# Fox attention scores for two heads at a time: three 64-row products per head on the two halves of the partitions

## The chip, the cores and the metric

The kernel runs on one core of a Trainium2 chip. The metric is the device time of one execution in microseconds (us); lower is better. The engines are named as the profile names them: PE is TensorE's matmuls and PEld its weight loads, DVE is VectorE, ACT is ScalarE, POOL is GpSimd, SP issues most of the transfers.

## What is computed

Two layers of a first block and one second block work on 512 tokens of 1024 features, all in float32. The change touches the attention of the first layer alone, which has 16 heads of 64 features and a forget gate:

```python
def _fox_attention(x, w_in, b_f, w_out):
    proj = x @ w_in
    q, k, v = ...                       # 16 heads of 64
    c = cumsum(log_sigmoid(f_logit))    # one running sum per head
    logits = einsum('bhqd,bhkd->bhqk', qb, k) * HEAD_DIM ** -0.5
    logits = logits + cb[..., :, None] - c[..., None, :]
    p = softmax(where(kpos <= qpos, logits, -inf))
    o = einsum('bhqk,bhkd->bhqd', p, v)
    return merge(o) @ w_out
```

Every product is made of float32 values split into a rounded part (hi) and the rest (lo), and leaves out the product lo x lo. So a product of two split operands has three terms: hi hi, hi lo, lo hi.

## The kernel before

The features lie on the partitions. `qk(pair)` projects q and k of two heads at once (48 matmuls of 512 columns, lines L217 to L219), so that head A lies on partitions 0 to 63 of the result and head B on 64 to 127. `qk_stack1` (L527) then makes three operands of the full height for each head: A holds q_hi on one half of the partitions and q_lo on the other, B holds k_hi on both halves, Ck holds k_lo on one half and zeros on the other. These zeros are set once by `zero_halves` (L506). A head takes three ACT and two DVE instructions of 64 partitions for it (L533 to L537).

`scores` (L540) is then two matmuls of the full 128 rows: A times B gives hi hi and lo hi together (L543), A times Ck gives hi lo (L544). There are four tiles of 128 queries; the keys of a tile are the causal ones, at least 256: 256, 256, 384 and 512 columns.

`fox_front` makes a head's gate row (L550, ACT copy L553, DVE sum L554), its scores, the row minima on DVE (L566, L569), the exponentials on ACT (L571) and the normalisation (L577 to L582). `fox_back` makes the transposes of the probabilities (L401), splits them (L193 on ACT, L194 on DVE) and multiplies with the values (L594, L595); `combine` (L604, L605) adds the two halves of its result.

The loop over heads in `fox` weaves the front of head h with the back of head h - 1. Projections for the next pair, the values (L291 to L293) and the first half of the output projection stand in the same program. A scheduler that is part of the build sets the order of the instructions on each engine from that program; the engines then run their queues in that order. Scores, gate rows and transposes use four PSUM banks in turns (`at`, 4 buffers), the product with the values uses one (`ms`), the projections three (`mm`). Inputs of the weight split are loaded by SP in chunks (`raw`, 3 buffers) and split by ACT and DVE (L185, L186).

`setup_cols` (L111) loads the small vectors into a staging tile `st`, transposes it (L156) and copies it to `cols`; this runs beside the first projections.

Of the kernel before, what the change touches and what calls it, by code (L numbers as in the profile page):

```python
# [15 lines left out]
S = 512  # L16
# [15 lines left out]
def constants():  # L32
    """Arrays that depend on shapes alone."""
# [36 lines left out]
def weave(*gens):  # L70
    """Runs generators step by step, in turns."""
    gens = [g for g in gens if g is not None]
    while gens:
        for g in list(gens):
            try:
                next(g)
            except StopIteration:
                gens.remove(g)


class K:
# [29 lines left out]
    def setup_cols(self):  # L111
# [26 lines left out]
        with self.tc.tile_pool(name="stage", bufs=1) as sp:  # L138
            r = 0
            st = None  # L140
            for name, ap, m in vecs:
                self.col[name] = r
                done = 0
                while done < m:
                    if r % P == 0:
                        st = sp.tile([P, P], F32, tag="st", name="st")
                        if total - r < P:
                            nc.vector.memset(st, 0.0)
                    k = min(m - done, P - r % P)
                    nc.sync.dma_start(st[r % P:r % P + k, :], ap[done * P:(done + k) * P].rearrange("(m p) -> m p", p=P))  # L150
                    done += k
                    r += k
                    if r % P == 0 or r == total:
                        b = (r - 1) // P
                        pt = self.psa()
                        nc.tensor.transpose(pt[:, :P], st, self.ident)  # L156
                        nc.vector.tensor_copy(self.cols[:, b * P:(b + 1) * P], pt[:, :P])
        # the gate of block 2's convolution takes halves
# [13 lines left out]
    def wchunk(self, src):  # L172
        """src [nk*128, cols] in DRAM, or a list of such to lie side by side; returns hi and lo tiles [128, nk, cols]."""
# [26 lines left out]
    def ws_load(self, W, c0, cols=256, ktiles=KD):  # L200
        """Chunks of W[:, c0:c0+cols] over K."""
# [19 lines left out]
    def ws_pairs(self, gc, vc, first):  # L221
        """Two pairs of products; the first ones after a new x^T by halves of the tokens."""
# [101 lines left out]
    def to_T(self, src, t):  # L324
        """src [128 tokens, 1024] -> xT[:, k, t*128:(t+1)*128]."""
# [30 lines left out]
    def rstd(self, var, eps, scale=1.0):  # L356
        """(var * scale + eps) ** -0.5 for a [128, n] tile."""
# [8 lines left out]
    def layer_norm(self, t, G, B, jk):  # L366
        """In place on x[:, t]; the row sums of its parts are in self.sums[t]; jk is scratch [128, 512]."""
# [15 lines left out]
    def res_epi(self, c0, n, scale, part=None, after=None):  # L383
        """x = scale * x + product; with part the row sums go to that column of self.sums."""
# [11 lines left out]
    def pT_split(self, Pt, j, t_from, pool, bufs=3):  # L396
        """Transposes of block column j of Pt[t] [128 q, keys] for t >= t_from, split into hi and lo."""
# [10 lines left out]
    def p_tile(self, pool, bufs=2):  # L408
        """Causal tiles of probabilities: for query tile t the keys up to (t + 1) * 128."""
# [4 lines left out]
    def fox(self, pool):  # L414
# [4 lines left out]
        # operands of the negated scores: [q_hi; q_lo], [k_hi; k_hi], [k_lo; 0] for each head of a pair  # L419
        Ck = self.zero_halves(pool)  # L420
# [13 lines left out]
        def qk(pair):  # L434
# [3 lines left out]
            o = self.qk_stack(qp, kp, pool, Ck, pair % 2)  # L438
            ops[2 * pair], ops[2 * pair + 1] = o
# [9 lines left out]

        def oproj(half, post=None):  # L450
# [3 lines left out]
        fx = [pool.tile([P, 1280], F32, tag="Pt", name="Pt", bufs=2) for _ in range(2)]  # L454
# [6 lines left out]
        # the first values and the forget gates' logits  # L461
# [9 lines left out]
        # v = log sigmoid; c = its running sum over the tokens  # L471
# [11 lines left out]
        self.setup_cols()  # L483
        prev = None
        for h in range(17):
            if h < 16:
                if h % 2 == 0 and h < 14:
                    qk(h // 2 + 1)
                if h in (1, 5, 9):
                    vproj(h // 4 + 1)  # L490
                Pt = self.p_tile(pool)
                cur = self.fox_front(pool, ops[h], h, sel, cst, causal, Pt)
            else:
                cur = None
            weave(cur, prev)
            prev = back(h, Pt) if h < 16 else None
            if h == 15:
                oproj(0)
        G, B = self.bcast(I["ln_attn_g"][0], "Pt", pool, 1280, 2), self.bcast(I["ln_attn_b"][0], "Pt", pool, 1280, 2)
        oproj(1, self.norm_post(G, B, pool.tile([P, S], F32, tag="NC", name="NC")))  # L500

# [7 lines left out]
    def log1pexp(self, a, b, c, d):  # L509
        """b = log(1 + exp(-|a|)); c, d scratch."""  # L510
# [36 lines left out]
    def fox_front(self, pool, ops, h, sel, cst, causal, Pt):  # L547
        nc = self.nc
        bp = self.psa()
        nc.tensor.matmul(bp, sel[:, h:h + 1].to_broadcast([P, P]), cst, start=True, stop=True)  # L550
        NC = pool.tile([P, S], F32, tag="NC", name="NC", bufs=1)
        BM = pool.tile([P, S], F32, tag="BM", name="BM", bufs=1)
        nc.scalar.activation(NC, bp, AF.Copy)  # L553
        nc.vector.tensor_tensor(out=BM.rearrange("p (t k) -> p t k", t=NT), in0=NC.rearrange("p (t k) -> p t k", t=NT),  # L554
                                in1=causal.rearrange("p (o k) -> p o k", o=1).to_broadcast([P, NT, P]), op=ALU.add)
        m1 = self.sm.tile([P, 4], F32, tag="m1", name="m1")
        m2 = self.sm.tile([P, 4], F32, tag="m2", name="m2")
        s4 = self.sm.tile([P, 4], F32, tag="s4", name="s4")
        yield
        for t in range(NT):  # L560
            n = (t + 1) * P
            sp = self.scores(ops, t, max(256, n))
            d = slice(t * P, n)
            init = -LOWEST
            if t:
                nc.vector.tensor_tensor_reduce(out=Pt[t][:, :t * P], in0=sp[:, :t * P], in1=NC[:, :t * P], scale=1.0, scalar=-LOWEST,  # L566
                                               op0=ALU.add, op1=ALU.min, accum_out=m1[:, t:t + 1])
                init = m1[:, t:t + 1]
            nc.vector.tensor_tensor_reduce(out=Pt[t][:, d], in0=sp[:, d], in1=BM[:, d], scale=1.0, scalar=init,  # L569
                                           op0=ALU.add, op1=ALU.min, accum_out=m2[:, t:t + 1])  # L570
            nc.scalar.activation(Pt[t], Pt[t], AF.Exp, scale=-1.0, bias=m2[:, t:t + 1], accum_out=s4[:, t:t + 1])  # L571
            yield
        self.normalise(Pt, s4)
# [25 lines left out]
    def combine(self, op, of, e, pool):  # L599
        """of rows of head e = upper + lower half of op."""  # L600
# [9 lines left out]
    def out_proj(self, W, k0, kt, xh, xl, scale, post=None):  # L610
        """x = scale * x + (rows k0.. of the product); the last part goes on to post(t)."""
# [12 lines left out]
    def xsn(self, groups, ktiles, xh, xl, k0=0):  # L624
        """As xs for groups (W, c0, epi) of 512 columns, by token tiles."""
# [122 lines left out]
    def softmax_exp(self, ops, Pt, mask):  # L748
        """Pt = exp(scores - max); returns 1 / sum."""
# [12 lines left out]
    def diff_front(self, ops1, ops2, mask, nlam, P1, P2, s1):  # L762
        """P1 = exp1 - lambda * sum1 / sum2 * exp2, which is sum1 times the difference; s1 gets the sums of exp1."""
# [9 lines left out]
    def diff_back(self, pool, P1, V, sg, oT, s1):  # L773
# [4 lines left out]
        for j in range(NT):  # L778
# [6 lines left out]
            if j == NT - 1:  # L785
                # o is s1 times the head's output
# [724 lines left out]
```

## Time and profile before

| | before |
|---|---|
| time, median of 3 runs | 2128.2 us (2127.27 to 2129.58) |
| profiled execution, first to last instruction (span) | 2127.1 us |
| PE busy | 2080.3 us, 98% |
| PEld busy | 1791.1 us, 84% |
| DVE busy | 1318.6 us, 62% |
| ACT busy | 1021.9 us, 48% |
| first and last gate row of the Fox heads (L550) start at | 63.6 and 228.2 us |

The profiled execution has no other time of its own than its span; the median of the runs is 1.1 us above it. "Busy" of PE counts matmuls until their modelled ends, which reach into the next matmul, so the step from one start to the next start, not the length of one matmul, says what a matmul costs on PE.

### The profile page before, as it was taken

What the parts mean: (1) busy time and instruction counts of PE and PEld (TensorE: products, weight loads), DVE (VectorE), ACT (ScalarE), POOL (GpSimd) and SP (SyncE); (2) the same over time, 40 slices, a digit from 0 to 9 for tenths busy, and PEclk for the clock granted to TensorE, in tenths of its full rate; (3) what the DMA queues carried; (4) which work ended last, traced back from release to release, by engine and by line L of the source; (5) the groups of instructions that cost most, each with busy time, mean ns of one, the idle gap of its engine ahead of it and who ended that gap; (6) DMA issues with size and microseconds to landing.
All of it is one profiled execution on the core that took longest, in us unless ns stands there. A gap on an engine that the chain in (4) does not pass through costs nothing.

```text
span 2127.1 us, 29643 instructions
## 1 busy us (share of the span) xinstructions
PE 2080.3 (98%) x11499; PEld 1791.1 (84%) x11499; DVE 1318.6 (62%) x2522; ACT 1021.9 (48%) x1880; POOL 74.3 (3%) x109
## 2 busy tenths in 40 slices
PE   8999999999999999999999998999999999999998
PEld 7888888898898788888998887877898778888887
DVE  5777876536636888775536547897798554332334
ACT  4777554314425987444324434676475343222322
POOL 0000000000000000010000001000000010000000
PEclk9999999999999999999999999999999999999999
DMA  6221233232323121252323323211323425232322
GB/s 167 61 60 60 70 126 109 92 97 80 107 82 100 50 70 60 65 165 79 102 87 109 94 91 106 70 30 35 104 61 96 138 94 172 87 104 84 114 92 72
DMA packets 206018, 193.82 MB, mean 91 GB/s; under 512 B 9029, under 2 KB 187446, under 8 KB 205878
## 3 DMA queue, kind: packets, MB, share of 16 engines
q1 hardware_dynamic: 199942, 173.04, 27.1%
q0 software_dynamic: 4928, 15.22, 2.3%
q10 hardware_dynamic: 1008, 3.67, 0.5%
q8 instruction: 91, 1.49, 0.3%
q14 instruction: 49, 0.40, 0.1%
HBM read 185.61 MB, written 6.29 MB: 90 GB/s over the span
## 4 chain that ended last, share of the span: by engine, by line
PE 51%; DVE 3%; ACT 1%; POOL 1%; issue 1%; POOLq 0%; DVEq 0%; ACTq 0%
PE mm L217 10%; PE mm L218 10%; PE mm L219 10%; PE mm L292 2%; PE mm L293 2%; PE mm L291 2%; PE mm L259 2%; PE mm L257 2%; PE mm L258 2%; PE at L1171 1%; PE at L259 1%; PE at L257 1%; PE at L401 1%; PE at L258 1%; DVE wlo L186 1%
## 5 line engine op out<-in xcount | busy, mean ns | idle before, releaser
L186 DVE TENSOR_TENSOR wlo<-raw,whi 128x1024 fp32r<-128x1024 f32 (+4 forms) x336 | 397.7, 1185 | 350.7 <-ACT whi L185 340.9
L217 PE MATMUL mm<-xTh,whi 128*128 128x512 f32 (+1 forms) x1584 | 604.7, 382 | 2.6 <-DVE L L1015 1.2
L219 PE MATMUL mm<-xTh,wlo 128*128 128x512 f32 (+1 forms) x1584 | 604.2, 382 | 0.1
L218 PE MATMUL mm<-xTl,whi 128*128 128x512 f32 (+1 forms) x1584 | 603.7, 381 | 0.0
L185 ACT ACTIVATE whi<-raw 128x1024 fp32r<-128x1024 f32 (+4 forms) x336 | 345.4, 1031 | 509.2 <-PE mm L218 209.4
L217 PEld LDWEIGHTS mm<-xTh,whi 128*128 128x128 f32 x1584 | 298.3, 188 | 57.6 <-issue 3.1
L219 PEld LDWEIGHTS mm<-xTh,wlo 128*128 128x128 f32 x1584 | 298.2, 188 | 56.1 <-DVE wlo L186 0.3
L218 PEld LDWEIGHTS mm<-xTl,whi 128*128 128x128 f32 x1584 | 298.5, 188 | 54.5 <-DVE xTl L194 0.2
L825 DVE SCALAR_TENSOR_TENSOR cy<-mm,cols,cy 128x511 f32<-128x511 f32 (+1 forms) x172 | 128.6, 748 | 108.4 <-ACT cy L823 105.5
L293 PE MATMUL mm<-whi,hl 128*128 128x256 f32 x528 | 149.4, 283 | 0.0
L292 PE MATMUL mm<-wlo,hh 128*128 128x256 f32 x528 | 149.4, 283 | 0.0
L291 PE MATMUL mm<-whi,hh 128*128 128x256 f32 x528 | 149.4, 283 | 0.0
L292 PE MATMUL mm<-wlo,xTh 128*128 128x256 f32 x416 | 118.4, 285 | 0.9 <-DVE wlo L186 0.9
L291 PE MATMUL mm<-whi,xTh 128*128 128x256 f32 x416 | 118.6, 286 | 0.3 <-ACT xTh L193 0.3
L293 PE MATMUL mm<-whi,xTl 128*128 128x256 f32 x416 | 118.0, 284 | 0.2 <-DVE xTl L194 0.2
L291 PEld LDWEIGHTS mm<-whi,hh 128*128 128x128 f32 x528 | 101.4, 192 | 0.2
L292 PEld LDWEIGHTS mm<-wlo,hh 128*128 128x128 f32 x528 | 101.4, 192 | 0.2
L293 PEld LDWEIGHTS mm<-whi,hl 128*128 128x128 f32 x528 | 101.4, 192 | 0.0
L823 ACT ACTIVATE cy<-mm,cols 128x512 f32<-128x512 f32 x86 | 66.2, 770 | 71.8 <-PE mm L219 71.8
L193 ACT ACTIVATE hh<-cy 128x512 fp32r<-128x512 f32 x66 | 41.1, 623 | 115.8 <-DVE cy L1398 58.9
L292 PEld LDWEIGHTS mm<-wlo,xTh 128*128 128x128 f32 x416 | 80.0, 192 | 1.9 <-DVE wlo L186 1.1
L291 PEld LDWEIGHTS mm<-whi,xTh 128*128 128x128 f32 x416 | 79.9, 193 | 1.5 <-ACT xTh L193 0.8
(422 smaller groups left out, 3580.6 us busy)
## 6 DMA issues: line engine op xcount, KB each, us to landing
raw<-in_ffn_w_in_dram SPq DMA_DIRECT2D x88, 512.0 KB
raw<-in_w_gate_up_dram SPq DMA_DIRECT2D x44, 512.0 KB
raw<-in_w_in_dram SPq DMA_DIRECT2D x40, 512.0 KB
raw<-in_ffn_w_out_dram SPq DMA_DIRECT2D x34, 512.0 KB
raw<-in_a_w_in_dram SPq DMA_DIRECT2D x22, 512.0 KB
raw<-in_w_down_dram SPq DMA_DIRECT2D x20, 512.0 KB
raw<-in_kv_w_dram SPq DMA_DIRECT2D x16, 512.0 KB
raw<-in_ffn_w_out_dram SPq DMA_DIRECT2D x12, 384.0 KB
```

The costliest lines, as they stand in the source:

```text
L185: nc.scalar.activation(hi, raw, AF.Copy)
L186: nc.vector.tensor_tensor(out=lo, in0=raw, in1=hi.bitcast(F32), op=ALU.subtract)
L217: mm(o, wh, a, start=(k == 0), stop=False)
L218: mm(o, wh, b, start=False, stop=False)
L219: mm(o, wl, a, start=False, stop=(k == ktiles - 1))
L257: mm(o, a, hi[:, kk, :], start=(k == 0), stop=False)
L258: mm(o, a, lo[:, kk, :], start=False, stop=False)
L291: mm(o, a, hi[:, kk, :], start=(k == 0 and t % 2 == 0), stop=False)
L292: mm(o, a, lo[:, kk, :], start=False, stop=False)
L293: mm(o, b, hi[:, kk, :], start=False, stop=(k == ktiles - 1 and t % 2 == 1))
L823: nc.scalar.activation(y, ps, AF.Identity, scale=self.c1(f"cw{l}2", m), bias=self.c1(f"cb{l}", m))
L825: nc.vector.scalar_tensor_tensor(out=y[:, o:], in0=ps[:, :S - o], scalar=self.c1(f"cw{l}{j}", m), in1=y[:, o:], op0=ALU.mult, op1=ALU.add)
```

## The change

The two heads of a pair go through `fox_front` together. q and k are split over the full height of 128 partitions into qh, ql, kh, kl, with one ACT and one DVE instruction each for both heads; the stacked operands and the zeros go. A head's scores are three products of 64 rows (qh kh, qh kl, ql kh), written in turns for the upper and the lower half of the partitions, into two PSUM banks. The backs of a pair are woven four steps at a time with the front of the next pair. Probability tiles have four buffers instead of two, gate rows two instead of one, and `setup_cols` uses the tile `of` for staging.

```diff
         def qk(pair):
...
-            o = self.qk_stack(qp, kp, pool, Ck, pair % 2)
-            ops[2 * pair], ops[2 * pair + 1] = o
+            o = ops[pair] = [pool.tile([P, S], F32R, tag=n, name=n, bufs=2) for n in ("qh", "ql", "kh", "kl")]
+            self.split(qp, o[0], o[1], scale=-0.125)
+            self.split(kp, o[2], o[3])
...
+        def backs(p, Pts):
+            for e in range(2):
+                yield from back(2 * p + e, Pts[e])
...
-        for h in range(17):
-            if h < 16:
-                if h % 2 == 0 and h < 14:
-                    qk(h // 2 + 1)
-                if h in (1, 5, 9):
-                    vproj(h // 4 + 1)
-                Pt = self.p_tile(pool)
-                cur = self.fox_front(pool, ops[h], h, sel, cst, causal, Pt)
...
-            weave(cur, prev)
-            prev = back(h, Pt) if h < 16 else None
-            if h == 15:
+        for p in range(9):
+            cur = None
+            if p < 8:
+                if p < 7:
+                    qk(p + 1)
+                if p in (1, 3, 5):
+                    vproj(p // 2 + 1)
+                Pts = [self.p_tile(pool, 4) for _ in range(2)]
+                cur = self.fox_front(pool, ops[p], p, sel, cst, causal, Pts)
+            weave(cur, self.bursts(prev, 4) if prev else None)
+            prev = backs(p, Pts) if p < 8 else None
+            if p == 7:
                 oproj(0)
...
         for t in range(NT):
             n = (t + 1) * P
-            sp = self.scores(ops, t, max(256, n))
+            sps = self.scores2(ops, t, max(256, n))
...
+    def scores2(self, ops, t, nk):
+
+        mm = self.nc.tensor.matmul
+        qh, ql, kh, kl = ops
+        sps = [self.psa(), self.psa()]
+        for i, (a, b) in enumerate(((qh, kh), (qh, kl), (ql, kh))):
+            for e in range(2):
+                r = slice(e * 64, (e + 1) * 64)
+                mm(sps[e][:, :nk], a[r, t * P:(t + 1) * P], b[r, :nk], start=(i == 0), stop=(i == 2))
+        return sps
```

The lines of the changed kernel after L111 stand elsewhere: the transposes are L400, the products with the values L617 and L618, the score products L595.

On PE, at the second head of the first pair, before: the score products (L543, L544; `at` is the score bank) stand between transposes (L401), and each tile has two of them behind each other.

```order
L543 MATMUL at_714<-B_399,A_398 128x256
L544 MATMUL at_714<-Ck10_154,A_398 128x256
L218 MATMUL mm_775<-xTl_77,whi_807 128x512
L401 MATMUL at_705<-ident_85,Pt_536 128x128 x3
L401 MATMUL at_719<-ident_85,Pt_536 128x128 x3
L543 MATMUL at_729<-B_399,A_398 128x256
L544 MATMUL at_729<-Ck10_154,A_398 128x256
L543 MATMUL at_735<-B_399,A_398 128x384
L544 MATMUL at_735<-Ck10_154,A_398 128x384
```

On PE, at the second tile of the second pair, now: `at_857` is the bank of the upper half's head and `at_858` that of the lower half's.

```order
L595 MATMUL at_857<-kh_506,qh_504 128x256
L595 MATMUL at_858<-kh_506,qh_504 128x256
L595 MATMUL at_857<-kl_507,qh_504 128x256
L595 MATMUL at_858<-kl_507,qh_504 128x256
L617 MATMUL ms_806<-ph_849,Vs_160 128x128
L595 MATMUL at_857<-kh_506,ql_505 128x256
L595 MATMUL at_858<-kh_506,ql_505 128x256
```

Here the halves take turns as in the code, with a product of another kind between the second and the third turn.

On PE, at the third tile of the same pair, now: `at_903` is the upper half's head, `at_904` the lower half's.

```order
L595 MATMUL at_903<-kh_506,qh_504 128x384
L595 MATMUL at_903<-kl_507,qh_504 128x384
L595 MATMUL at_903<-kh_506,ql_505 128x384
L218 MATMUL mm_958<-xTh_76,wlo_962 128x512
L216 MATMUL mm_958<-xTh_76,whi_961 128x512
L217 MATMUL mm_958<-xTl_77,whi_961 128x512
L617 MATMUL ms_874<-ph_880,Vs_160 128x512
L218 MATMUL mm_958<-xTh_76,wlo_962 128x512
L216 MATMUL mm_958<-xTh_76,whi_961 128x512
L618 MATMUL ms_874<-pl_881,Vs_160 128x512
L617 MATMUL ms_874<-ph_888,Vs_160 128x384
L595 MATMUL at_904<-kh_506,qh_504 128x384
```

Here the scheduler has moved the three products of the upper half together, and those of the lower half come after seven products of the full height. Behind the Fox stage the order on every engine is that of before.

## Rows read from the trace of the kernel before

**Rows 1.** The page, part 1: busy us (share of the span) xinstructions.

```profile
PE 2080.3 (98%) x11499; PEld 1791.1 (84%) x11499; DVE 1318.6 (62%) x2522; ACT 1021.9 (48%) x1880; POOL 74.3 (3%) x109
```

**Rows 2.** Windows: us, busy (x) of PE, PEld, DVE, ACT, POOL, PEclk, DMA share, GB/s.

```profile
63.60:246.30 182.70, 179.90 (x1097) 154.78 (x1096) 149.31 (x441) 136.69 (x324) 0.54 (x1) 1.00 0.20 59
```

**Rows 3.** Lines of PE, 63.6 to 246.3 us: line, tiles, shapes, count, busy, mean ns, idle before.

```profile
L543 PE MATMUL at<-B,A 128*128 128x256 f32 (+1 forms) x64 | 23.1, 365 | 1.7 <-ACT NC L553 1.6
...
L544 PE MATMUL at<-Ck,A 128*128 128x256 f32 (+1 forms) x64 | 20.7, 324 | 0.0
```

**Rows 4.** Timeline of PE in the first head's scores: start us, us, instruction.

```profile
64.01 0.28 PE L544 MATMUL at<-Ck,A 128*128 128x256 f32 x1
64.12 0.29 PE L543 MATMUL at<-B,A 128*128 128x256 f32 x1
...
64.56 0.34 PE L544 MATMUL at<-Ck,A 128*128 128x384 f32 x1
64.74 0.39 PE L219 MATMUL mm<-xTh,wlo 128*128 128x512 f32 x1
...
65.20 0.39 PE L543 MATMUL at<-B,A 128*128 128x512 f32 x1
65.43 0.40 PE L544 MATMUL at<-Ck,A 128*128 128x512 f32 x1
```

**Rows 5.** Timeline of PEld around a transpose of the first projections.

```profile
40.08 0.19 PEld L217 LDWEIGHTS mm<-xTh,whi 128*128 128x128 f32 x1
40.19 0.19 PEld L218 LDWEIGHTS mm<-xTl,whi 128*128 128x128 f32 x1
```

**Rows 6.** Timeline of PE in block 2: four transposes onto 128, then onto 32 columns.

```profile
1406.22 0.60 PE L947 MATMUL at<-ident,L 128*128 128x128 f32 x4
1406.57 0.48 PE L217 MATMUL mm<-xTh,whi 128*128 128x512 f32 x1
...
1407.35 0.61 PE L1080 MATMUL ms<-ident,L 128*32 128x128 f32 x4
1407.71 0.48 PE L217 MATMUL mm<-xTh,whi 128*128 128x512 f32 x1
```

**Rows 7.** Timeline of PE around the transpose of [rows 5].

```profile
40.08 0.27 PE L156 MATMUL at<-ident,st 128*128 128x128 f32 x1
40.10 0.48 PE L217 MATMUL mm<-xTh,whi 128*128 128x512 f32 x1
40.42 0.40 PE L218 MATMUL mm<-xTl,whi 128*128 128x512 f32 x1
```

**Rows 8.** Waits of PEld, 63.6 to 246.3 us: waiter, releaser, us, times, longest.

```profile
PEld ms L594 <- ACT ph L193: 4.2, 13, 0.7
PEld at L543 <- ACT NC L553: 3.6, 6, 0.8
PEld at L401 <- ACT Pt L580: 2.7, 8, 0.6
PEld ms L595 <- DVE pl L194: 1.3, 5, 0.5
```

**Rows 9.** Lines of DVE and of ACT, 63.6 to 246.3 us.

```profile
L194 DVE TENSOR_TENSOR pl<-at,ph 128x512 fp32r<-128x512 f32 x15 | 10.3, 685 | 0.3 <-ACT ph L193 0.3
...
L534 DVE SCALAR_TENSOR_TENSOR A<-mm,A 64x512 fp32r<-64x512 f32 x12 | 8.3, 689 | 1.6 <-ACT A L533 1.3
L537 DVE TENSOR_TENSOR Ck<-mm,B 64x512 fp32r<-64x512 f32 x12 | 8.3, 689 | 5.4 <-ACT B L536 4.6 <-PE at L401 0.7
...
L193 ACT ACTIVATE ph<-at 128x512 fp32r<-128x512 f32 x15 | 8.8, 590 | 2.2 <-PE at L401 2.2
...
L536 ACT ACTIVATE B<-mm 64x512 fp32r<-64x512 f32 x12 | 7.1, 594 | 0.1
```

**Rows 10.** Lines of DVE and of PE, 0 to 28 us.

```profile
L506 DVE MEMSET Ck<- 128x512 f32 x4 | 1.9, 485 | 0.2
...
L330 PE MATMUL at<-ident,x 128*128 128x128 f32 x32 | 6.5, 389 | 8.7 <-DMA x<-in_x_dram 8.7
```

More of the change, by code (lines that the diff above doesn't have):

```diff
@@ L109, in setup, with setup_cols @@
         nc.vector.memset(self.mhalf, -0.5)
-    def setup_cols(self):
+    def setup_cols(self, pool):
         nc, const, I = self.nc, self.const, self.I
@@ L137, in setup_cols @@
         self.col = {}
[L138 to L157, printed above, removed]
+        r = 0
+        st = None
+        for name, ap, m in vecs:
+            self.col[name] = r
+            done = 0
+            while done < m:
+                if r % P == 0:
+                    st = pool.tile([P, S], F32, tag="of", name="of", bufs=1)[:, :P]
+                    if total - r < P:
+                        nc.vector.memset(st, 0.0)
+                k = min(m - done, P - r % P)
+                nc.sync.dma_start(st[r % P:r % P + k, :], ap[done * P:(done + k) * P].rearrange("(m p) -> m p", p=P))
+                done += k
+                r += k
+                if r % P == 0 or r == total:
+                    b = (r - 1) // P
+                    pt = self.psa()
+                    nc.tensor.transpose(pt[:, :P], st, self.ident)
+                    nc.vector.tensor_copy(self.cols[:, b * P:(b + 1) * P], pt[:, :P])
         i = self.col["c2w0"]
@@ L418, in fox @@
         oT = {}
-        Ck = self.zero_halves(pool)
         Vq, ops, of = {}, {}, {}
@@ L452, in oproj @@
                           1.0 if half else ALPHA, post)
-        fx = [pool.tile([P, 1280], F32, tag="Pt", name="Pt", bufs=2) for _ in range(2)]
+        fx = [pool.tile([P, 1280], F32, tag="Pt", name="Pt", bufs=4) for _ in range(2)]
         v, b, c, d = (fx[1][:, i * 64:(i + 1) * 64] for i in range(4))
@@ L482, in fox @@
         qk(0)
-        self.setup_cols()
+        self.setup_cols(pool)
         prev = None
-        for h in range(17):
-            if h < 16:
-                if h % 2 == 0 and h < 14:
-                    qk(h // 2 + 1)
-                if h in (1, 5, 9):
-                    vproj(h // 4 + 1)
-                Pt = self.p_tile(pool)
-                cur = self.fox_front(pool, ops[h], h, sel, cst, causal, Pt)
-            else:
-                cur = None
-            weave(cur, prev)
-            prev = back(h, Pt) if h < 16 else None
-            if h == 15:
+        for p in range(9):
[10 more added lines that the diff above has]
+            if p == 7:
                 oproj(0)
-        G, B = self.bcast(I["ln_attn_g"][0], "Pt", pool, 1280, 2), self.bcast(I["ln_attn_b"][0], "Pt", pool, 1280, 2)
-        oproj(1, self.norm_post(G, B, pool.tile([P, S], F32, tag="NC", name="NC")))
+        G, B = self.bcast(I["ln_attn_g"][0], "Pt", pool, 1280, 4), self.bcast(I["ln_attn_b"][0], "Pt", pool, 1280, 4)
+        oproj(1, self.norm_post(G, B, pool.tile([P, S], F32, tag="NC", name="NC", bufs=2)))
     def zero_halves(self, pool):
@@ L545, in scores, with fox_front @@
         return sp
-    def fox_front(self, pool, ops, h, sel, cst, causal, Pt):
+    def fox_front(self, pool, ops, pair, sel, cst, causal, Pts):
         nc = self.nc
[L549 to L558, printed above, removed]
+        mm = nc.tensor.matmul
+        NCs, BMs, m1, m2, s4 = [], [], [], [], []
+        for e in range(2):
+            h = 2 * pair + e
+            bp = self.psa()
+            mm(bp, sel[:, h:h + 1].to_broadcast([P, P]), cst, start=True, stop=True)
+            NC = pool.tile([P, S], F32, tag="NC", name="NC", bufs=2)
+            BM = pool.tile([P, S], F32, tag="BM", name="BM", bufs=2)
+            nc.scalar.activation(NC, bp, AF.Copy)
+            nc.vector.tensor_tensor(out=BM.rearrange("p (t k) -> p t k", t=NT), in0=NC.rearrange("p (t k) -> p t k", t=NT),
+                                    in1=causal.rearrange("p (o k) -> p o k", o=1).to_broadcast([P, NT, P]), op=ALU.add)
+            NCs.append(NC)
+            BMs.append(BM)
+            m1.append(self.sm.tile([P, 4], F32, tag="m1", name="m1"))
+            m2.append(self.sm.tile([P, 4], F32, tag="m2", name="m2"))
+            s4.append(self.sm.tile([P, 4], F32, tag="s4", name="s4"))
         yield
@@ L561, in fox_front @@
             n = (t + 1) * P
-            sp = self.scores(ops, t, max(256, n))
+            sps = self.scores2(ops, t, max(256, n))
             d = slice(t * P, n)
[L564 to L571, printed above, removed]
-            yield
-        self.normalise(Pt, s4)
+            for e in range(2):
+                sp, Pt, NC, BM = sps[e], Pts[e], NCs[e], BMs[e]
+                init = -LOWEST
+                if t:
+                    nc.vector.tensor_tensor_reduce(out=Pt[t][:, :t * P], in0=sp[:, :t * P], in1=NC[:, :t * P], scale=1.0, scalar=-LOWEST,
+                                                   op0=ALU.add, op1=ALU.min, accum_out=m1[e][:, t:t + 1])
+                    init = m1[e][:, t:t + 1]
+                nc.vector.tensor_tensor_reduce(out=Pt[t][:, d], in0=sp[:, d], in1=BM[:, d], scale=1.0, scalar=init,
+                                               op0=ALU.add, op1=ALU.min, accum_out=m2[e][:, t:t + 1])
+                nc.scalar.activation(Pt[t], Pt[t], AF.Exp, scale=-1.0, bias=m2[e][:, t:t + 1], accum_out=s4[e][:, t:t + 1])
+            yield
+        for e in range(2):
+            self.normalise(Pts[e], s4[e])
+    def scores2(self, ops, t, nk):
[3 more added lines that the diff above has]
+        for i, (a, b) in enumerate(((qh, kh), (qh, kl), (ql, kh))):
+            for e in range(2):
+                r = slice(e * 64, (e + 1) * 64)
+                mm(sps[e][:, :nk], a[r, t * P:(t + 1) * P], b[r, :nk], start=(i == 0), stop=(i == 2))
+        return sps
     def normalise(self, Pt, s4):
@@ L1357, in steps, with bursts @@
     @staticmethod
+    def bursts(gen, n):
+        for i, _ in enumerate(gen):
+            if i % n == n - 1:
+                yield
+    @staticmethod
     def steps(gen, n):
```

## The prediction

> **What bounds the kernel now.** I read the page's busy times first [rows 1]: PE is busy for 98% of the span, DVE for 62%, ACT for 48%. Then the windows, because an average says nothing of one stage. Behind the Fox stage the order of the instructions is the same in both kernels, so what the change does is decided there, and I take the stretch from the first gate row to the start of the second output projection [rows 2]: 182.7 us, of which PE is busy 179.9, DVE 149.3 and ACT 136.7, at a granted clock of 1.00, the 2.4 GHz level. So PE is the bound in this stage as well, with 2.8 us of open idle time; projections fill it whenever the attention is not ready. What the stage costs is then the sum of the steps of PE's queue, start to start, plus waits. That makes the score products count in full: a matmul more there is a matmul later at the end. The timeline gives the steps [rows 4]: 0.11 to 0.13 us for 256 columns (I take 0.12; the rows give 64.01 to 64.12), 0.18 for 384 (64.56 to 64.74), 0.23 for 512 (65.20 to 65.43). A weight load follows another after 0.11 us where nothing else holds it [rows 5], so at 256 columns load and product are about level.
>
> **The score products.** The lines count 64 + 64 of them before [rows 3], which is 16 heads times four tiles (256, 256, 384, 512 columns) times two: 64 of 256, 32 of 384, 32 of 512. By the steps that is 64 x 0.12 + 32 x 0.18 + 32 x 0.23 = 7.7 + 5.8 + 7.4 = 20.8 us. After, three products per tile and head: 96 x 0.12 + 48 x 0.18 + 48 x 0.23 = 11.5 + 8.6 + 11.0 = 31.2 us. If each 64-row product takes the array as long as a 128-row product of the same columns, the change adds **10.4 us**. What was one matmul of the full height (hi hi and lo hi in one) has become two of half the height, and that is a loss unless the halves run at the same time.
>
> **What the halves can give back.** No product of before uses only half of the rows, so the trace does not show whether two of them overlap; I bound it. The lower bound is nothing. For the upper bounds I went through the order of the changed kernel: of the 192 products, neighbours on different halves can be matched in 25 pairs of 256 columns, 4 of 384 and 17 of 512; the rest stand behind a product of the same half or of the full height, because the scheduler has moved the turns apart. If a pair costs one step, the gain is 25 x 0.12 + 4 x 0.18 + 17 x 0.23 = 3.0 + 0.7 + 3.9 = 7.6 us. If the weight loads of the two still follow each other at 0.11 us, a pair takes at least 0.22, and the gain is 25 x 0.02 + 4 x 0.14 + 17 x 0.23 = 0.5 + 0.6 + 3.9 = 5.0 us. I take **-5.0 us**: the products use different rows and different banks, but the step of the loads is in the rows of this trace and I see nothing that removes it. The Trainium skill, "TensorEngine Tiling (Array Packing)", section Key Properties, says that different tiles can execute weight loads and matmuls in parallel; by that the gain would be 7.6 us, and no run here has shown it.
>
> **Changing between 128 and 64 rows.** The 192 products stand in 68 runs between matmuls of the full height, so the array changes its division 136 times. The nearest rows are the four transposes onto 32 columns in block 2 [rows 6]: they and the change back take 1407.35 to 1407.71, 0.36 us, against 0.35 for four of the full width just before (1406.22 to 1406.57). That is a change of columns and not of rows, but it is the only one in the trace and it costs at most 0.01 us. The other end of the bound is that the array runs empty at every change: a matmul of 256 columns lasts 0.28 us and its successor starts 0.11 to 0.12 after it [rows 4], so about 0.16 us would be open each time, 136 x 0.16 = 21.8 us. I take 0. The same page of the Trainium skill, in the same section, says that changing the tiling mode drains TensorE; [rows 6] do not agree with it for columns, and for rows nothing here tells. By that rule the sum below would be higher by up to those 21.8 us.
>
> **Fewer ends of transpose groups.** A matmul behind a transpose group starts its successor late: 40.10 to 40.42 is 0.32 us for 512 columns against 0.23 [rows 7 and 4]. The groups of L401 number 64 in the order before and 46 after, since a pair's backs come in larger pieces. 18 x 0.09 = **-1.6 us**. Between 0 and -1.6, since some groups also hide a wait.
>
> **Splits of q and k.** Before, a head takes two DVE (0.69 us) and three ACT instructions (0.59) of 64 partitions; now a pair takes two and two of 128 partitions, which last as long: 0.685 and 0.59 [rows 9]. Per pair DVE goes from 2.76 to 1.37 us, ACT from 3.55 to 1.18; over eight pairs 11 us of DVE and 19 of ACT. On the path this costs and brings nothing, because PE is what the stage waits for: DVE has 33 us open in the stretch and ACT 46. It can only come back through PE's waits.
>
> **PE's waits.** Weight loads waited 4.2 + 3.6 + 2.7 + 1.3 = 11.8 us for ACT and DVE in the stretch [rows 8]; most of that lies under the matmul that is still running, since PE's open idle time is 2.8 us. Lighter ACT and DVE would shorten these waits. But the new order makes others. A pair needs two of the four `at` banks per tile; the next tile's two products wait until DVE has read the minima of both heads and split a transpose that has a third bank, and behind the waiting product in PE's queue stand the products with the values, for which `ms` and then the next head's back wait. The transposes of the second head of a pair come right behind those of the first, with one `ms` bank for both, so that the second product group waits for ACT's and DVE's `combine` (512 columns each, by [rows 9] about 0.6 and 0.7 us). Fillers are used less evenly: about 14 of the 48 projections of a pair stand inside the woven part and the others behind it in one piece. From below I bound the sum of it at -11.8 us (all of [rows 8] goes), from above at +8 x 1.3 = +10.4 (one unhidden `combine` per pair). I take **+1.5 us**, close to no change, since all of before's waits in the open amount to 2.8.
>
> **At no cost.** The four memsets of 485 ns that go stand in the first 28 us, where PE waits 8.7 us for x [rows 10]; with that cover gone they would be worth 1.9 us. The staging tile moves to `of`, with one buffer as before, and in PE's order its five transposes still have some 18 to 37 projections of 512 columns between them (4.1 to 8.5 us at 0.23). The extra buffers of Pt and NC remove waits for space that do not appear among PE's. The projections of a third pair now stand ahead of the first front and the values behind it: the same instructions.
>
> **Sum.** 10.4 - 5.0 - 1.6 + 1.5 = +5.3 us on the span of 2127.1, or 2132.4; the median of the runs is 1.1 us above that span, so I forecast **2133.5 us**, 0.25% slower. What a measurement here can tell from no change is about 0.2%, 4.3 us.
>
> **Rivals.**
> - *No overlap.* The halves run behind each other. For it: no row shows an overlap, and 55 of the neighbours among the products are of the same half. 10.4 - 1.6 + 1.5 = +10.3: 2138.5 us. Chance 0.24.
> - *Every change of rows empties the array.* For it: 136 changes, 0.16 us open at the most; against it [rows 6]. With half to all of the price on top of the forecast +16 to +27: 2144 to 2155 us. Chance 0.13. The skill's rule on the drain, named above, would give this.
> - *Full overlap, loads too.* 10.4 - 7.6 - 1.6 + 1.5 = +2.7: 2131 us, no change that can be told. Against it the 0.11 us between loads [rows 5]. Chance 0.10.
> - *The lighter ACT and DVE free PE's queue* (the other side): the waits of [rows 8] go instead of growing. 10.4 - 5.0 - 1.6 - 11.8 = -8.0: 2120 us. It decides once more than 8.1 of the 11.8 us come back as time. For it: ACT and DVE lose 30 us of work in the stretch. Against it: the open idle time is only 2.8 us, so most of the 11.8 is already hidden. Chance 0.15.
>
> **From the cases to the numbers.** The forecast itself has 0.38, within about 2129 to 2138. It is slower by more than 0.2% about six times in ten, else the same; no overlap and the emptied array are slower nearly always, full overlap is the same mostly, the freed queue is faster mostly. That makes slower 0.61, same 0.26, faster 0.13. The range from 2123 to 2147 leaves out about half of the freed queue and the upper part of the emptied array.
>
> **What would show it.** After, the 192 products of L595: the step between neighbours on different halves. 0.22 to 0.23 us for a pair of 512 columns shows overlap, 0.46 shows none; for a pair of 256, 0.22 shows that loads follow each other, 0.12 that they don't. The step over a change from a full-height product to a half-height one: more than the column step by 0.1 or so shows an emptied array. PE's and PEld's waits on ACT ph, on DVE's minima and on the gate rows in the stretch show the wait term, and the start of the first product of the second output projection, 246.3 us in [rows 2], shows the sum: some 5 us later. Behind it both traces should run alike. The prediction is wrong if the stretch changes by less than 2 us or by more than 12, or if the difference comes from a place behind it.

## The result and the profile after

The changed kernel takes 2146.6 us (median of 4 runs, 2145.3 to 2148.6) against 2128.45 (2127.3 to 2129.6) of the kernel before, run beside it: a ratio of 1.0086, 95% interval [1.0074, 1.0098], or +18.1 us. The forecast was 2133.5, +5.3. The profiled span is 2144.7 us, 17.6 more than before.

The page, part 1, after. Against [rows 1] PE has 21 us more and 64 more matmuls, DVE 13 and ACT 21 us less:

```profile
PE 2101.5 (98%) x11563; PEld 1796.7 (84%) x11563; DVE 1305.9 (61%) x2502; ACT 1001.0 (47%) x1848; POOL 74.1 (3%) x109
```

The stretch of [rows 2], from the first gate row to the first product of the second output projection, after (windows, the columns of [rows 2]):

```profile
63.00:263.00 200.00, 199.99 (x1188) 161.10 (x1188) 140.01 (x426) 120.08 (x298) 1.06 (x2) 1.00 0.20 59
```

200.0 us in place of 182.7: 17.3 of the 17.6 us lie here, at the same granted clock of 1.00 (2.4 GHz). PE no longer has any open idle time (199.99 of 200.00), and DVE and ACT are busy less than before. So PE does not stand idle for the engines that supply it; it steps more slowly itself. The waits of PEld in that stretch, to be held against [rows 8]:

```profile
PEld at L595 <- issue: 4.8, 20, 0.4
PEld ms L618 <- issue: 1.8, 7, 0.4
PEld mm L218 <- issue: 1.5, 5, 0.4
PEld at L595 <- ACT NC L560: 1.4, 6, 0.2
```

Before, every wait of note ended with ACT or DVE. Now the longest end with "issue": the load waited for nothing that the profile shows. The timeline of PE in the first, third and fourth tile of the first pair shows where (start us, us; an x2 row is two instructions of one kind):

```profile
63.69 0.39 PE L595 MATMUL at<-kh,qh 64*128 64x256 f32 x2
63.91 0.28 PE L595 MATMUL at<-kl,qh 64*128 64x256 f32 x2
64.03 0.28 PE L595 MATMUL at<-kh,ql 64*128 64x256 f32 x2
...
66.30 0.28 PE L290 MATMUL mm<-whi,xTh 128*128 128x256 f32 x1
66.42 0.28 PE L291 MATMUL mm<-wlo,xTh 128*128 128x256 f32 x1
66.63 0.45 PE L595 MATMUL at<-kh,qh 64*128 64x384 f32 x2
66.91 0.34 PE L595 MATMUL at<-kl,qh 64*128 64x384 f32 x2
67.08 0.35 PE L595 MATMUL at<-kh,ql 64*128 64x384 f32 x2
67.35 0.38 PE L292 MATMUL mm<-whi,xTl 128*128 128x256 f32 x1
67.67 0.50 PE L595 MATMUL at<-kh,qh 64*128 64x512 f32 x2
68.00 0.39 PE L595 MATMUL at<-kl,qh 64*128 64x512 f32 x2
68.23 0.40 PE L595 MATMUL at<-kh,ql 64*128 64x512 f32 x2
68.56 0.38 PE L290 MATMUL mm<-whi,xTh 128*128 128x256 f32 x1
68.78 0.28 PE L291 MATMUL mm<-wlo,xTh 128*128 128x256 f32 x1
68.90 0.28 PE L292 MATMUL mm<-whi,xTl 128*128 128x256 f32 x1
```

Two things are to be read here. **The halves overlap:** the two products of 512 columns at 68.00 are followed by the next two after 0.23 us, and the two of 256 columns at 63.91 after 0.12, each time the step of one (the trace has the two at 68.00 0.004 us apart). By the prediction's own sign, 0.12 for a pair of 256 says that the loads of the two do not follow each other either. **Every change of row division costs twice.** The step into it is longer: 66.42 to 66.63 is 0.21 us for 256 columns in place of 0.12, 68.23 to 68.56 is 0.33 for 512 in place of 0.23. And the step after the first product of the new division is longer too: 66.63 to 66.91 is 0.28 for 384 in place of 0.17 or 0.18, 67.67 to 68.00 is 0.33 in place of 0.23, 68.56 to 68.78 is 0.22 in place of 0.12. The lone projection at 67.35 stands between two changes and pays for both: 0.32 us in place of 0.12. PEld's timeline of the same place shows more:

```profile
67.35 0.19 PEld L292 LDWEIGHTS mm<-whi,xTl 128*128 128x128 f32 x1 [0.25 <-issue]
67.66 0.18 PEld L595 LDWEIGHTS at<-kh,qh 64*128 64x128 f32 x2
67.77 0.19 PEld L595 LDWEIGHTS at<-kl,qh 64*128 64x128 f32 x2
68.00 0.19 PEld L595 LDWEIGHTS at<-kh,ql 64*128 64x128 f32 x2
68.56 0.19 PEld L290 LDWEIGHTS mm<-whi,xTh 128*128 128x128 f32 x1 [0.36 <-issue]
68.67 0.19 PEld L291 LDWEIGHTS mm<-wlo,xTh 128*128 128x128 f32 x1
```

Within one division a load runs under the matmul ahead of it: the load for 68.00 starts at 67.77, that for 68.78 at 68.67. Across a change it does not: the load of L290 starts at 68.56, with its own matmul, when the products of 68.23 have been streamed and 0.10 more has passed. Over the stretch the load of a first product starts 0.002 us ahead of it, that of any other 0.118 (medians). The step behind the first product is longer by about the same 0.10 whether it has 256 columns or 512, though a second load, 0.11 behind the first ([rows 5]), would fit under 512 columns (0.23). So it is the first product's own load that nothing hides. This is argued from the steps; the trace does not show when the array begins to multiply.

I added this up over the whole stretch: the step from each matmul's start to the next, less the step that its columns cost undisturbed (0.227, 0.173, 0.120 and 0.067 us for 512, 384, 256 and 128 columns), sorted by where the matmul stands.

| part of the stretch, us | before | after | difference |
|---|---|---|---|
| columns of all matmuls | 163.3 | 172.3 | +9.0 |
| products that start together (44 pairs) | 0 | -7.1 | -7.1 |
| changes of division: step into, step out, the step behind each (136) | 0 | 27.1 | +27.1 |
| steps behind transposes | 5.7 | 2.6 | -3.1 |
| all other steps | 13.7 | 5.0 | -8.7 |
| stretch | 182.7 | 199.9 | +17.2 |

The stretch does not hold quite the same work twice: the 64 more score products are 10.2 us of columns, and the rest has 1.2 us less (48 products of 512 columns and 14 shorter ones have left it, 90 of 256 columns have come into it).

27.1 us over 136 changes is 0.20 us each, and that price hardly scatters: a matmul between two changes takes 0.19 us beyond its columns (median of 44), so few waits are hidden in it. The last rows say that PE, slowed down, waits less for ACT and DVE.

### The profile page after: what moved, and what is told of

It reads as the page before. It is cut to its first block, busy times and chain, and to the rows that moved or that the text cites. A ratio compares the mean times of both kernels' runs of the same rounds, so it can differ in the third digit from the quotient of the medians.

```text
span 2144.7 us, 29749 instructions
## 1 busy us (share of the span) xinstructions
PE 2101.5 (98%) x11563; PEld 1796.7 (84%) x11563; DVE 1305.9 (61%) x2502; ACT 1001.0 (47%) x1848; POOL 74.1 (3%) x109
## 4 chain that ended last, share of the span: by engine, by line
PE 50%; DVE 3%; ACT 1%; POOL 1%; issue 1%; POOLq 0%; DVEq 0%; ACTq 0%
PE mm L216 10%; PE mm L217 10%; PE mm L218 10%; PE mm L291 2%; PE mm L292 2%; PE mm L290 2%; PE mm L258 2%; PE mm L257 2%; PE mm L256 2%; PE at L1194 1%; PE at L258 1%; PE at L257 1%; PE at L400 1%; PE at L256 1%; DVE wlo L185 1%
## 5 line engine op out<-in xcount | busy, mean ns | idle before, releaser
L290 PE MATMUL mm<-whi,hh 128*128 128x256 f32 x528 | 149.4, 283 | 0.0
L290 PE MATMUL mm<-whi,xTh 128*128 128x256 f32 x416 | 118.0, 285 | 0.3 <-ACT xTh L192 0.2
L290 PEld LDWEIGHTS mm<-whi,hh 128*128 128x128 f32 x528 | 101.4, 192 | 0.2
L290 PEld LDWEIGHTS mm<-whi,xTh 128*128 128x128 f32 x416 | 79.7, 192 | 1.9 <-ACT xTh L192 0.7
```

What stands on the lines that cost most here:

```text
L290: mm(o, a, hi[:, kk, :], start=(k == 0 and t % 2 == 0), stop=False)
```

## The experiments

Theory 1: each change between 128 and 64 rows costs PE a fixed price, and pairs overlap in full. Its rivals: the pairwise order costs the time (2), or the columns of the third product do (3).

**The changes alone.** The kernel before, with the second product on the 64 rows that are not zero:

```diff
+        r = slice(0, P) if e is None else slice(e * 64, (e + 1) * 64)
...
-        self.nc.tensor.matmul(sp[:, :nk], A[:, t * P:(t + 1) * P], Cc[:, :nk], start=False, stop=True)
+        self.nc.tensor.matmul(sp[:, :nk], A[r, t * P:(t + 1) * P], Cc[r, :nk], start=False, stop=True)
```

> The kernel before, with only the second product of each score tile (q stack times [k_lo; 0]) restricted to the 64 rows of its head; the 64 rows left out held zeros, so the same is computed, with the same number of products, columns and groups, and no pairs. The 64 products stand alone among products of the full height: 64 runs, 128 changes of row division, no neighbours on different halves. Theory 1 (each change between 128 and 64 rows costs PE 0.15 to 0.2 us: the next division waits for the array to empty, and its second weight load is no longer hidden): +19 to +26 us, 2147 to 2154 us. Theory 2 (changes are free; the pairwise order with its bunched backs costs the time): no change, 2126 to 2131. Theory 3 (changes are free, the columns of the third product cost it): no change, 2126 to 2131.

Measured: 2146.9 us against 2128.8, ratio 1.0084 [1.0069, 1.0099]. With no pair structure, no third product and no other split, 128 changes alone bring +18.1 us, so they are enough for a slowdown of this size. That it is the same 18.1 as in the changed kernel is chance: there columns and overlap count as well. What the order and the columns add is measured below. The timeline of PE at the place of [rows 4]:

```profile
63.58 0.28 PE L544 MATMUL at<-B,A 128*128 128x256 f32 x1
63.79 0.38 PE L545 MATMUL at<-Ck,A 64*128 64x256 f32 x1
64.10 0.38 PE L544 MATMUL at<-B,A 128*128 128x256 f32 x1
64.41 0.38 PE L545 MATMUL at<-Ck,A 64*128 64x256 f32 x1
64.72 0.45 PE L544 MATMUL at<-B,A 128*128 128x384 f32 x1
```

63.79 to 64.10 to 64.41 to 64.72: every product between two changes takes 0.31 us in place of 0.12, so 0.19 for each change. Over the stretch the same sum as above gives 27.0 us for 128 changes, 0.21 each; the other steps fall from 13.7 to 6.5, though ACT and DVE do exactly what they did before, and the steps behind transposes from 5.7 to 3.4, since some of these now end at a change and are counted with it. 27.0 - 7.2 - 2.3 is the 17.5 us by which the stretch grows: 27 us come out as 18, or 0.14 for each change.

**How the price adds up.** The same edit for two of the four tiles of each head:

```diff
-            sp = self.scores(ops, t, max(256, n))
+            sp = self.scores(ops, t, max(256, n), h % 2 if t < 2 else None)
```

> As the run with the second product on 64 rows, but only for the first two tiles of each head (256 columns): 32 lone products of 64 rows, 64 changes of row division in place of 128. The run with 128 changes came out 18.1 us over the kernel before, 0.14 us for each change. Theory 1 (a fixed price for each change): 64 x 0.14 = 9 us, 2136 to 2139 us (0.19 each, as single steps show, would give 2141). Rival (the price belongs to the long products, or comes from something else that the 64-row products disturb): no change or nearly the whole 18 us, that is 2128 to 2131 or 2145 and more.

Measured: 2135.2 us, 1.0032 [1.0020, 1.0043], +6.8 us, a little under the 2136 to 2139 of Theory 1. And with `t >= 2`:

> The other half of the run with two tiles: the second product on 64 rows for the third and fourth tile of each head alone (384 and 512 columns): 32 lone products, 64 changes. If the prices simply add, 18.1 - 6.8 = 11.3 us over before, 2139 to 2141 us, 0.18 for each change. If every change costs the same 0.14 us and the run with 256 columns was low by scatter: 9 us, 2137. If a change behind longer products waits longer (the array takes longer to empty): more than 11, 2141 or above.

Measured: 2137.7 us, 1.0043 [1.0031, 1.0056], +8.5 us. On PE the price is about the same in both (14.9 us for 64 changes, 0.23 each; 12.2, 0.19 each); long products don't pay more. The 0.23 holds 2.0 us of late steps behind transposes, which fall from 5.7 to 3.7 there; a matmul between two changes pays 0.19 in both. The two halves bring 15.3 us together and the whole 18.1: either half alone takes some of the same waits away (the other steps fall by 6.1 and by 3.1 us from 13.7, by 7.2 with all changes), and a wait can go only once. So neither simple addition nor 0.14 for each change holds exactly after these waits.

**Rows or columns.** My zero came from a change of columns [rows 6]. Here the second product has the full rows and 64 columns of the array:

```diff
+            self.nc.tensor.matmul(sp[:, :nk], A[:, t * P:(t + 1) * P], B[:, :nk], start=True, stop=True)
+            self.nc.tensor.matmul(sp[:m, :nk], A[:, t * P:t * P + m], B[:, :nk], start=True, stop=True)
```

> The kernel before, with the second product of each score tile over the full 128 rows but onto only 64 columns (64 of the 128 queries): 64 lone products, 128 changes of the columns' division, the rows never divided. The product repeats the first one for those queries, so the term of k_lo is left out of the scores; the number of products and their streamed columns are those of before. Theory 1 as the forecast had it from the transposes onto 32 columns (a change of columns is free, only a change of rows costs): 2126 to 2131 us. Rival (any change of division costs the same 0.14 us as rows): 2145 to 2149.

Measured: 2128.7 us against 2129.2, 0.9998 [0.9989, 1.0007]. The timeline, same place:

```profile
63.92 0.28 PE L544 MATMUL at<-B,A 128*128 128x256 f32 x1
64.04 0.28 PE L545 MATMUL at<-B,A 128*64 128x256 f32 x1
64.16 0.28 PE L544 MATMUL at<-B,A 128*128 128x256 f32 x1
64.28 0.28 PE L545 MATMUL at<-B,A 128*64 128x256 f32 x1
64.41 0.45 PE L544 MATMUL at<-B,A 128*128 128x384 f32 x1
```

Steps of 0.12 throughout. Going between products onto 128 and onto 64 columns is free, going between 128 and 64 rows is not. The times of [rows 6] were read rightly and were about something else. The Trainium skill, "TensorEngine Tiling (Array Packing)", section Key Properties, says that changing the tiling mode drains TensorE. The 0.10 us ahead of each change of rows agree with it. Onto 64 columns nothing of the kind shows; but the profile names the rows and columns that a product uses and not the mode of the array, so whether the mode changed there is not shown, neither here nor in [rows 6].

**The pair structure without half rows.** The fronts of two heads together, with the stacked operands of before (room made by two buffers less and by a `combine` that writes through its output tile):

```diff
-            sps = self.scores2(ops, t, max(256, n))
+            sps = [self.scores(ops[e], t, max(256, n)) for e in range(2)]
```

> The pairwise structure of the changed kernel (fronts of two heads together, bursts of four steps, four Pt buffers) with the stacked operands of the kernel before: two products of the full height per tile and head, so no change of row division at all. To make room for the stacks, the combine of a head writes through its own output tile and two buffer counts are one lower. Theory 1: the time of before less the gains on waits and transpose groups, 2122 to 2130 us. Theory 2: the time of the changed kernel or near it, 2140 to 2147. Theory 3: near before, 2126 to 2131.

Measured: 2130.9 us, 1.0011 [1.0001, 1.0020], just above the range of Theory 1, within that of Theory 3 (near before) and far below Theory 2, which is out. The structure itself brings no gain: its steps behind transposes fall by 2.3 us, but its other steps rise from 13.7 to 18.1, with waits for ACT such as these (waits of PEld, 62.6 to 246.2):

```profile
PEld at L400 <- ACT NC L559: 4.3, 4, 2.2
PEld ms L616 <- ACT ph L192: 4.2, 15, 0.4
```

**Three products without half rows.** Each q operand of the full height, with zeros in the other head's half:

```diff
-                mm(sps[e][:, :nk], a[r, t * P:(t + 1) * P], b[r, :nk], start=(i == 0), stop=(i == 2))
+                mm(sps[e][:, :nk], a[e][:, t * P:(t + 1) * P], b[:, :nk], start=(i == 0), stop=(i == 2))
...
```

> The changed kernel with its three products per head, but each q operand is of the full height with zeros in the other head's half, so that all products have 128 rows: the same columns (96 more than... three per tile and head), no change of row division and no two products at once. Same room made as in the run with stacks. Theory 1: before plus 10.4 us of columns less 2 to 5 us of waits and groups: 2133 to 2137 us, that is 10 us below the changed kernel although nothing overlaps. Theory 2: 2150 or more (structure cost kept and the overlap lost). Theory 3 (columns cost the time, nothing overlaps): 2145 to 2149.

Measured: 2134.5 us, 1.0027 [1.0017, 1.0037], +5.6, as Theory 1 has it; Theory 3 (2145 to 2149) is out. The same products, none of them at the same time as another, are 12 us faster than the changed kernel: the halves cost more than they give back.

**The control** for the room made in these two:

```diff
-        nc.scalar.activation(sh[m], op[o], AF.Copy)
-        nc.vector.tensor_tensor(out=of[m], in0=op[m], in1=sh[m], op=ALU.add)
+        nc.scalar.activation(of[m], op[o], AF.Copy)
+        nc.vector.tensor_tensor(out=of[m], in0=op[m], in1=of[m], op=ALU.add)
...
```

> Control: the changed kernel with nothing but the room made as in the two runs before it (the combine through the output tile, two buffer counts one lower). 73 runs of half-height products instead of 68, 146 changes instead of 136; matched neighbours 23, 2 and 17 instead of 25, 4 and 17. All theories: 2145 to 2150 us; Theory 1 adds 1.5 to 2.5 us to the changed kernel's 2146.6 for ten more changes and three fewer matches.

Measured: 2153.5 us, 1.0113 [1.0096, 1.0130], 6.9 above the changed kernel; I expected 1.5 to 2.5. Its stretch runs from 66.78 to 270.10:

```profile
66.78:270.10 203.32, 203.24 (x1188) 162.75 (x1188) 140.82 (x427) 120.39 (x298) 1.08 (x2) 0.99 0.19 58
```

The stretch is 3.4 us longer than the changed kernel's, 2.5 of it by 146 changes in place of 136. It also starts 3.7 us later, which belongs to the order of the work ahead of it; I did not look into that, and this miss stays open. In the two runs above the stretch starts as early as in the changed kernel (62.6 and 63.0). The control came out slower, not faster, so nothing suggests that the room made those two look better.

**Fewer changes.** The six products of a tile ahead of other ready work, in their written turns:

```diff
+        with self.tc.high_priority():
...
+                    if (i, e) != (0, 0):
+                        self.tc.keep_in_program_order(m)
```

> The changed kernel with the six products of a tile put ahead of other ready work and in their written turns: 53 runs in place of 68, that is 106 changes, and 40, 17 and 16 matched neighbours of 256, 384 and 512 columns in place of 25, 4 and 17. Theory 1: 30 changes less at 0.14 to 0.19 us is -4.2 to -5.7, more overlap is 11.5 - 7.6 = -3.9: 8 to 10 us below the changed kernel, 2137 to 2139. Rival (order doesn't matter, the columns cost the time): 2145 to 2148. Rival (putting the scores ahead delays the work that DVE and ACT need next): 2148 or more.

Measured: 2137.8 us, 1.0043 [1.0030, 1.0055], 8.8 below the changed kernel, as Theory 1 has it: 106 changes cost 21.9 us in place of 27.1, and 71 products start together (-10.7 in place of -7.1).

**Turns or no turns.** The written order kept without priority, the halves in turns:

```diff
-            for e in range(2):
+            for e in (1, 0):
...
+                if (i, e) != (0, 1):
+                    self.tc.keep_in_program_order(m)
```

> The changed kernel with its products kept in written turns of the two halves, without putting them ahead of other work: 78 runs (156 changes), 35, 17 and 16 matched neighbours. Theory 1: 20 changes more at 0.14 to 0.19 us is +2.8 to +3.8, overlap 4.2 + 3.1 + 3.7 = 11.0 in place of 7.6 is -3.4: about the changed kernel, 2145 to 2148. Rival without overlap or without a price for changes: 2143 or less, or 2150 and more.

Measured: 2146.4 us, 1.0083 [1.0069, 1.0097], as Theory 1 has it. And head by head:

```diff
+        for e in (1, 0):
+            for i, (a, b) in enumerate(((qh, kh), (qh, kl), (ql, kh))):
...
```

> As the run with written turns, also 78 runs and 156 changes, but the three products of one head behind each other: 7, 1 and 8 matched neighbours of 256, 384 and 512 columns in place of 35, 17 and 16. The two runs differ in little but the overlap. Theory 1 with full overlap of neighbours on different halves (matmul and weight load): 11.0 - 2.8 = 8 us above the run with turns, 2153 to 2156. Rival (loads still follow each other at 0.11 us, as the forecast had it): 28 x 0.02 + 16 x 0.14 + 8 x 0.23 = 4.6 us above it, 2150 to 2151. Rival (no overlap): the same as with turns.

Measured: 2153.0 us, 1.0116 [1.0102, 1.0129], 6.6 above the run with turns, between full overlap (8) and loads that follow each other (4.6). The changes cost the same on PE (30.8 and 30.0 us for 156), the products that start together 4.3 and 10.1. The order head by head got more overlap than its neighbours allow, 24 pairs that start together where 16 are neighbours; its timeline shows how:

```profile
67.77 0.51 PE L595 MATMUL at<-kh,qh 64*128 64x512 f32 x2
68.11 0.40 PE L595 MATMUL at<-kl,qh 64*128 64x512 f32 x2
68.34 0.40 PE L595 MATMUL at<-kh,ql 64*128 64x512 f32 x2
```

In this kernel's program the three products of one head (kh qh, kl qh, kh ql) stand ahead of the three of the other, yet both heads' kh qh start at 67.77. The trace has starts alone; the order of PE's queue is taken from the program.

**As few changes as can be.** The six products held together as one piece:

```diff
+        with self.tc.tile_critical():
```

> The changed kernel with the six products of every tile held together as one piece that nothing may enter: 32 runs, 64 changes, and all 48, 24 and 24 neighbours of 256, 384 and 512 columns matched. To hold them together each piece begins and ends with an instruction of PE's sequencer, 64 in all, which no run so far prices. Theory 1 without a price for these: from the run with the products put ahead (2137.8, 106 changes, overlap 11.5): 42 changes less at 0.14 us is -5.9, overlap 15.6 - 11.5 = -4.1, so 2128 us, equal to before. Theory 1 with 0.1 to 0.2 us for each of the 64: 2134 to 2141. Rival (the held piece keeps other engines waiting, a wait in place of the changes): 2145 or more.

Measured: 2182.3 us, 1.0247 [1.0233, 1.0261]. Theory 1's numbers failed and the last rival was right. The waits of PEld in its stretch (63 to 299 us), and of DVE:

```profile
PEld at L596 <- issue: 41.9, 32, 4.9
```

```profile
DVE Pt L577 <- PEq L592: 60.3, 22, 6.0
```

The piece waits with everything behind it on PE, 32 times and up to 4.9 us, and DVE waits for it. 92 products start together here (-14.4 us), but the steps into the 32 pieces cost 37.2 us beyond their columns. This run prices the holding, not the changes.

## Why the prediction came out as it did

The direction was right, and the time lies in the range, 0.4 us under its upper edge, but the mechanism was wrong, and that the range held is luck. The changes alone would have put the forecast at 2160.6 us; a wait term that missed by 10.2 the other way and three smaller misses brought it back. By the prediction's own sign (wrong if the stretch changes by more than 12 us) it failed: the stretch grew by 17.3. The likeliest case, 2129 to 2138, was not what happened; the rival "every change of rows empties the array" was, which had 0.13 and 2144 to 2155 us.

- **Changing between 128 and 64 rows (taken as 0): the step that failed.** It measures +27.1 us on PE, 0.20 for each of 136 changes, and 0.19 to 0.23 in each of the other kernels with half rows, the held pieces aside; a matmul between two changes pays 0.191 to 0.195 in all of them (medians). I judged it by the nearest rows, which were of another kind: products onto fewer columns, which the run with 64 columns confirms as free. ([rows 6] is not the only such place: four transposes onto 16 columns stand at 35.3 us of the same trace.) My upper bound, 0.16 for each change (+21.8), was too low for PE as well: it had the emptying, which measures 0.09 to 0.10 and not 0.16, but not the first product's own load, another 0.10 that nothing hides.
- **What the halves give back (-5.0): mis-sized.** 44 pairs start together, weight loads too, and give 7.1 us; the step of 0.11 between loads [rows 5] does not hold across halves. The Trainium skill, "TensorEngine Tiling (Array Packing)", section Key Properties, says that different tiles can load and multiply in parallel. These 44 pairs agree with it.
- **The score products (+10.4): right.** The 64 more products are 10.2 us of columns (+9.0 for the stretch in all, since its other work is 1.2 less), and three products of full height without overlap come to +5.6 us in the run with zeros, the smaller waits taken off.
- **PE's waits (+1.5): wrong sign.** The other steps fall by 8.7 us. A slower PE alone can do most of that: in the run of the changes alone, with the work of ACT and DVE as before, they fall by 7.2. The fear that the new order makes waits was right by itself: with the stacked operands they rise by 4.4. In the run with zeros, of the same order but with ACT's work 12.3 us lighter in the stretch and PE's columns 9.0 longer, they fall by 2.2. How the 8.7 divide between PE coming later and lighter ACT and DVE stays open.
- **Ends of transpose groups (-1.6):** -3.1; some of the groups now end at a change and are counted there.
- **Splits, memsets and staging at no cost:** no run prices them alone, and nothing speaks against it; the first gate row starts 0.5 us earlier than before. ACT and DVE lose 16.6 and 9.3 us in the stretch ([rows 2] and the window after), and no kernel came out faster.

By the measured terms the sum is 9.0 - 7.1 + 27.1 - 3.1 - 8.7 = +17.2. Set at nothing was one term alone of this size; the one on the waits took a third of it back.

No run came out faster than the kernel before. An estimate from the steps on PE, before anything comes back from waits: with a tile's six products in one run, the 32 tiles would cost 31.2 / 2 = 15.6 us and 64 changes of 0.20, 12.8: 28.4 in place of the 20.8 of two stacked products. Even two tiles to a run (not tried) would have 15.6 + 6.4 = 22.0.

## What to carry to other kernels

Products of 64 rows on the two halves run at the same time, loads and all, but each passage between them and products of 128 rows costs PE about 0.2 us, as much as a product of about 450 columns (0.227 us for 512). Count the runs of half-height products in the order of the changed kernel, not the products: here a run had fewer than three (192 in 68), and every run brings two changes. Where a zero block makes the height full, ask first what taking it out saves: here leaving it in was 18 us faster (the changes alone). And where the nearest row of a trace is of another kind than the thing to be priced (columns for rows), keep the other bound as likely. A time inside a wide range is no sign that the terms were right.

## What the runs showed of the hardware that I had not expected

- A change of rows costs in two places, 0.10 us ahead of the first product and 0.10 behind it, and the load of the new division does not start under the old one's matmul. Together they are 0.191 to 0.195 us (median for a matmul between two changes) in all eight kernels with half rows, the held pieces aside. Products onto 64 columns among products onto 128 (128 times there or back) cost nothing: 0.9998 [0.9989, 1.0007].
- The halves do not seem bound to the order in which they are written: with three products of one half written ahead of three of the other, the first of each start 0.01 us apart, and the other two follow in step (67.77, 68.11, 68.34 above).
- A slower PE pays for part of itself. 27 us of changes came out as 18 in the run of the changes alone: 7.2 us of other steps, waits for ACT and DVE among them, went (2.3 more are transposes' late steps that are counted with the changes), in a kernel where PE is busy for 98% of the time.
